# FFN up: products 1, 6, 7 and 4 add up in one accumulator pair, with ScalarE copies of the states between

## Chip, core, metric

One core of one Trainium2 chip runs the whole program in one launch. The metric is device microseconds of that core; the time of a kernel is the median of its runs. All five engines have their own instruction stream and wait for one another by semaphores: TensorE (PE in the profile) multiplies, VectorE (DVE), ScalarE (ACT), GpSimd (POOL) and SyncE (SP), which here only issues DMAs.

## The reference, cut to what matters

Two layers of a decoder trunk with 512 tokens and 1024 features, all in float32. Each layer is a mixer of four branches, which is not touched, and then the feed-forward network (FFN) with 2816 hidden features:

```python
hf = rmsnorm(x, norm_ffn)
gate, up = jnp.split(hf @ ffn_w_up, 2, axis=-1)
return x + (jax.nn.silu(gate) * up) @ ffn_w_down
```

The change lies in `hf @ ffn_w_up`: (512 x 1024) times (1024 x 5632), and in the silu and the product behind it.

## The kernel before

**Precision.** A float32 product is made of three TensorE matmuls, `mm3` (lines 306, 307, 308): each operand is split into hi and lo, and hi·hi, lo·hi and hi·lo are added. The weights are split on the core: ScalarE copies the raw float32 weights into `w_hi` (line 118, the helper of all activations), VectorE subtracts that from them into `w_lo` (line 1212 in the FFN, line 270 elsewhere).

**Products.** The up projection is not made of eight block products (two halves of the tokens by two halves of the features by gate and up) but of seven, in the manner of Strassen and Winograd, on sums of blocks. The inputs are `h` (`h_hi`, `h_lo`) and sums of its blocks, `sx` (`s_hi`, `s_lo`, whose lo is made on line 1134). The weight blocks are summed too: a `Block` is loaded by SP (line 1188), a second matrix is added to it by an accumulating DMA on GpSimd's queue (line 1193) or by VectorE (`plus`, line 1203). The hidden features are taken in six groups q, five of 512 columns and a last one of 256. Of each group:

- `X` begins as gate weights plus up weights of the even rows, `Y` as the up weights of the odd rows. X plus Y feeds p6, and later, with the gate weights of the odd rows (`w`) added to it, p4. Y alone feeds p3; with the even rows' up weights added to it by DMA it feeds p7. X at first feeds p5.
- p1 takes the gate weights of the even rows, p2 those of the odd rows, `w`.

A product is 24 matmuls: two token blocks t, four row blocks k, three of `mm3`, in two halves of two k each, since a weight block is split in two pieces (four pieces are kept, `W_BUFS`, and three raw buffers `w_raw`, `RAW_BUFS`; two more raw buffers `f_raw` belong to the FFN's own pool and take the place of the mixer's memory).

**Accumulators.** The FFN has four pairs of PSUM banks: A, B, C, and tr for transposes. The products of a group run p1, p6, p3, p2, p7, then the transposes of the first two token blocks' result (`turn`, on line 1264, with a VectorE part on line 1268), then p5 of the next group, then p4. p1 and p2 add up in A; p6, p7 and p4 in B; p5 and p3 in C (in the last group p4 uses C). VectorE makes the sums that leave PSUM (`plus` on line 1359): p1 plus C into e, p1 plus B into u, u plus C, e plus B, and p1 plus B behind p4; ScalarE copies p1 out once (into d1). u and e are the up parts; gate parts go through ScalarE's silu, with the norm's factor as its scale, and VectorE multiplies (`silu_mul`, line 1329).

**Order.** The program is written in the order above, but a scheduler with a simulated timeline puts each engine's instructions in their order when the program is built; weight splits and the additions behind products have a raised priority. After groups 2 and 5 the down projection takes the groups so far (`a_hi`, `a_lo`).

Of the kernel before, what the change touches and what calls it, by code (L numbers as in the profile page):

```python
# [16 lines left out]
AF = mybir.ActivationFunctionType  # L17
OP = mybir.AluOpType
# [52 lines left out]
def hybrid_trunk(ctx: ExitStack, tc: tile.TileContext, x, mem, positions, norm_mix, w_in, conv_w,  # L71
# [92 lines left out]
    ps = tr_ps()  # L164
# [1053 lines left out]
    def ffn(l, h, sx, ssq, xr, spare, late):  # L1218
# [2 lines left out]
        widths = [512] * (FF // 512) + [FF % 512]  # L1221
        Q = len(widths)
        ends = {2: (0, 3), Q - 1: (3, Q)}
        HS = S // 2
        A11, S1, A12, A22, S3, S2, S4 = ((h, 0, 0), (h, 0, HS), (h, 1, 0), (h, 1, HS), (sx, None, 0), (sx, None, HS),
                                         (sx, None, 2 * HS))

        with tc.tile_pool(name="ffn", bufs=1) as fp:
            a = (fp.tile([P, 12, S], F32R, name="a_hi"), fp.tile([P, 12, S], F32R, name="a_lo"))
            norm = {}  # L1230

            def block(n, name="w_raw"):
                if name == "w_raw":
                    t = wpool.tile([P, 2048], F32, name="w_raw", bufs=RAW_BUFS)
                else:
                    t = fp.tile([P, 2048], F32, name=name, bufs=2)
                return Block(t[:, :4 * n].rearrange("p (k n) -> p k n", n=n), n)

            def gate_w(q):
                return up[:, q * 512:q * 512 + widths[q]]  # L1240

            def up_w(q):
                return up[:, FF + q * 512:FF + q * 512 + widths[q]]

            def product(pss, form, parts, first, mid=None):
                src, odd, s0 = form
                n = parts[0][0].shape[2]
                for i, (hi, lo) in enumerate(parts):
                    for t in range(2):
                        for k in range(2):  # L1250
                            kk = 2 * i + k
                            c = kk if odd is None else 2 * kk + odd
                            mm3(pss[t][:, :n], pair(src, c, slice(s0 + t * P, s0 + (t + 1) * P)),
                                (hi[:, k, :], lo[:, k, :]), first and kk == 0, kk == 3, not first)
                    if i == 0 and mid is not None:
                        mid()

            def turn(tiles, t0, q):
                n = widths[q]
                base = 4 * (q % 3)  # L1260
                for t, src in enumerate(tiles):
                    ps = tr_ps()
                    for i in range(n // P):
                        pe.transpose(ps[:, i * P:(i + 1) * P], src[:, i * P:(i + 1) * P], ident)  # L1264
                    ps = ps[:, :n].rearrange("p (a b) -> p a b", b=P)
                    hi, lo = (x[:, base:base + n // P, (t0 + t) * P:(t0 + t + 1) * P] for x in a)
                    A(hi, ps, AF.Copy)
                    dve.tensor_sub(lo, ps, f(hi))

            def tmps(i, n):  # L1270
                return [spare[:, 2 * i + t, :n] for t in range(2)]

            def accs(name):
                return [bank[name]() for _ in range(2)]

            st = {}

            def first_sum(q):
                urgent = ()
                if q:  # L1280
                    moves = st[q - 1]["Y"].moves
                    urgent = (moves[2:], order) if q == 1 else (moves[:2], landed)
                if q == 0:
                    st[q] = {"B11": block(widths[q]).load(gate_w(q), 0), "X": block(widths[q])}
                else:
                    st[q] = {"X": block(widths[q], "f_raw")}
                st[q]["X"].load(gate_w(q), 0).add(up_w(q), 0, *urgent)

            def p5(q):
                d = st[q]  # L1290
                d["C"] = accs("C")
                product(d["C"], S1, d["X"].split(*zip(*st[q - 1]["g"]) if q else ()), True)

            def p1(q, mid=None):
                d = st[q]
                d["A"] = accs("A")
                w = d["B11"] if q == 0 else block(widths[q]).load(gate_w(q), 0)
                product(d["A"], A11, w.split(), True, mid)

            def p6(q):  # L1300
                d = st[q]
                d["B"] = accs("B")
                d["Y"] = block(widths[q]).load(up_w(q), 1)
                d["X"].plus(d["Y"])
                product(d["B"], S2, d["X"].split(), True)

            def p3(q):
                d = st[q]
                product(d["C"], S4, d["Y"].split(), False)
                d["Y"].add(up_w(q), 0)  # L1310

            def p2(q):
                d = st[q]
                w = block(widths[q], "w_raw" if q else "f_raw").load(gate_w(q), 1)
                product(d["A"], A12, w.split(), False)
                d["X"].plus(w)

            def p7(q):
                product(st[q]["B"], S3, st[q]["Y"].split(), False)

            def p4(q):
                d = st[q]
                if q == Q - 1:
                    d["C"] = accs("C")
                product(d["BC"[q == Q - 1]], A22, d["X"].split(), q == Q - 1)

            def silu_mul(dst, src, t, other):
                return (A(dst, src, AF.Silu, scale=norm["r"][:, t:t + 1]),
                        dve.scalar_tensor_tensor(dst, other, norm["n"][:, t:t + 1], dst, op0=OP.mult, op1=OP.mult))

            pending = []

            def flush():
                for args in pending:
                    turn(*args)
                pending.clear()

            def hi_prio():
                return tc.high_priority(offset=AHEAD)

            def down(q):
                g0, g1 = ends[q]
                f0, f1 = g0 * 512, min(g1 * 512, FF)
                kt = (f1 - f0) // P
                wd = ffn_w_down[l][f0:f1, :]
                end = q == Q - 1
                if last:
                    down_tokens(xr, wd, a, kt, end)
                    return None, None
                h2 = ssq2 = None  # L1350
                if end:
                    h2, ssq2 = new_h(), new_ssq()
                residual(lambda m: xr[:, m, :], wd, a, kt, 256, h2, ssq2, lambda c: g_mix(l + 1, c), spill=end)
                return h2, ssq2

            def plus(dst, src, ps, n):
                with hi_prio():
                    for t in range(2):
                        dve.tensor_add(dst[t], src[t], ps[t][:, :n])

            first_sum(0)
            for q in range(Q):
                n = widths[q]
                d1, e, u, g = (tmps(i, n) for i in ((0, 1, 2, 3) if q % 2 else (3, 1, 2, 0)))
                p1(q, flush)
                d = st[q]
                if q == 0:
                    p5(0)
                    late()
                    r = norm_token(ssq)  # L1370
                    nr = small(NT, name="nrstd_t", bufs=2)
                    dve.tensor_scalar(nr, r, -1.0, None, op0=OP.mult)
                    norm.update(r=r, n=nr)
                with hi_prio():
                    for t in range(2):
                        A(d1[t], d["A"][t][:, :n], AF.Copy)
                plus(e, d1, d["C"], n)
                p6(q)
                plus(u, d1, d["B"], n)
                p3(q)  # L1380
                if q + 1 < Q:
                    first_sum(q + 1)
                plus(u, u, d["C"], n)
                p2(q)
                d["g"] = [silu_mul(g[t], d["A"][t][:, :n], t, u[t]) for t in range(2)]
                p7(q)
                plus(e, e, d["B"], n)
                turn(g, 0, q)
                if q + 1 < Q:
                    p5(q + 1)  # L1390
                if q + 1 == Q:
                    plus(d1, d1, d["B"], n)
                p4(q)
                plus(d1, d1, d["BC"[q + 1 == Q]], n)
                for t in range(2):
                    silu_mul(d1[t], d1[t], t + 2, e[t])
                pending.append((d1, 2, q))
                if q in ends:
                    flush()
                    res = down(q)  # L1400
# [40 lines left out]
```

## Time and profile before

| what | value |
|---|---|
| median of 3 runs | 1996.49 us (1995.89 to 1996.67) |
| span of the profiled execution | 1994.9 us, granted TensorE clock 1.000 |
| the profiled execution against the runs | its span is 1.6 us below their median; the profile gives no time beyond the span |
| busy: TensorE, VectorE, ScalarE, GpSimd | 100%, 70%, 52%, 4% |
| the FFN of layer 0 in that span | about 682 to 968 us and the down projection's end behind it |
| the FFN of layer 1 | begins at about 1649 us |

In a timeline row stand the start in us, the busy us, the engine, the line, the operation, output and inputs, and the count; in brackets the idle time ahead of it and what ended it. In a group's row stand the count, the busy us and the mean ns of one, then the engine's idle time ahead of these instructions. A waits row has the total us, the number of times and the longest. TensorE's rows overlap, since matmuls are pipelined: what a matmul costs in a stream is the distance between two starts.

### The profile page before, as it was taken

What the parts mean: (1) busy time and instruction counts of PE and PEld (TensorE: products, weight loads), DVE (VectorE), ACT (ScalarE), POOL (GpSimd) and SP (SyncE); (2) the same over time, 40 slices, a digit from 0 to 9 for tenths busy, and PEclk for the clock granted to TensorE, in tenths of its full rate; (3) what the DMA queues carried; (4) which work ended last, traced back from release to release, by engine and by line L of the source; (5) the groups of instructions that cost most, each with busy time, mean ns of one, the idle gap of its engine ahead of it and who ended that gap; (6) DMA issues with size and microseconds to landing.
All of it is one profiled execution on the core that took longest, in us unless ns stands there. A gap on an engine that the chain in (4) does not pass through costs nothing.

```text
span 1994.9 us, 26474 instructions
## 1 busy us (share of the span) xinstructions
PE 1987.4 (100%) x10057; PEld 1669.8 (84%) x10057; DVE 1394.2 (70%) x2661; ACT 1033.3 (52%) x1795; POOL 69.9 (4%) x85
## 2 busy tenths in 40 slices
PE   9999999999999999999999999999999999999999
PEld 7898988778888888888889898877888888888897
DVE  7779997547666887458657889853677578854772
ACT  7653643666553645234555454366767455532551
POOL 1000000000000010000000000000000001100100
PEclk9999999999999999999999999999999999999999
DMA  9632223213234485353453223321322346643541
GB/s 314 208 106 75 76 88 103 67 53 104 66 99 144 114 202 138 116 148 75 131 165 95 81 63 96 95 85 53 96 85 76 118 145 171 152 143 106 116 128 53
DMA packets 172498, 226.86 MB, mean 114 GB/s; under 512 B 5954, under 2 KB 120212, under 8 KB 172372
## 3 DMA queue, kind: packets, MB, share of 16 engines
q1 hardware_dynamic: 155072, 193.55, 30.2%
q0 software_dynamic: 13344, 23.21, 7.2%
q10 hardware_dynamic: 3956, 8.42, 1.1%
q8 instruction: 79, 1.29, 0.3%
q14 instruction: 47, 0.39, 0.1%
HBM read 214.67 MB, written 10.49 MB: 113 GB/s over the span
## 4 chain that ended last, share of the span: by engine, by line
PE 98%; DMA 1%; ACT 0%; DVE 0%; SPq 0%; issue 0%; DVEq 0%; ACTq 0%
PE mm L306 19%; PE mm L307 19%; PE mm L308 18%; PE B L306 5%; PE B L307 5%; PE B L308 5%; PE A L308 4%; PE A L307 4%; PE A L306 4%; PE C L306 2%; PE C L307 2%; PE C L308 2%; PE tr L797 1%; PE tr L1264 1%; PE tr L791 1%; PE at L767 1%
## 5 line engine op out<-in xcount | busy, mean ns | idle before, releaser
L118 ACT ACTIVATE w_hi<-w_raw 128x1024 fp32r<-128x1024 f32 (+1 forms) x362 | 373.2, 1033 | 415.9 <-PE mm L307 149.4
L270 DVE TENSOR_TENSOR w_lo<-w_raw,w_hi 128x1024 fp32r<-128x1024 f32 x258 | 311.8, 1209 | 180.4 <-ACT w_hi L118 178.1
L306 PE MATMUL mm<-h_hi,w_hi 128*128 128x512 f32 x960 | 377.5, 394 | 1.3 <-DVE gate L596 0.9
L307 PE MATMUL mm<-h_lo,w_hi 128*128 128x512 f32 x960 | 377.0, 393 | 0.0
L308 PE MATMUL mm<-h_hi,w_lo 128*128 128x512 f32 x960 | 375.4, 392 | 0.0
L306 PEld LDWEIGHTS mm<-h_hi,w_hi 128*128 128x128 f32 x960 | 180.4, 188 | 39.1 <-DVE gate L596 1.3
L307 PEld LDWEIGHTS mm<-h_lo,w_hi 128*128 128x128 f32 x960 | 180.4, 188 | 36.7 <-issue 1.5
L308 PEld LDWEIGHTS mm<-h_hi,w_lo 128*128 128x128 f32 x960 | 180.4, 188 | 36.2 <-issue 0.2
L1212 DVE TENSOR_TENSOR w_lo<-w_raw,w_hi 128x1024 fp32r<-128x1024 f32 (+1 forms) x104 | 118.4, 1140 | 43.7 <-ACT w_hi L118 43.0
L306 PE MATMUL mm<-w_hi,h_hi 128*128 128x256 f32 (+2 forms) x384 | 116.3, 304 | 0.0
L307 PE MATMUL mm<-w_lo,h_hi 128*128 128x256 f32 (+2 forms) x384 | 116.2, 303 | 0.0
L308 PE MATMUL mm<-w_hi,h_lo 128*128 128x256 f32 (+2 forms) x384 | 116.1, 302 | 0.0
L308 PE MATMUL mm<-y_hi,w_lo 128*128 128x512 f32 x256 | 100.5, 393 | 0.0
L306 PE MATMUL mm<-y_hi,w_hi 128*128 128x512 f32 x256 | 100.3, 393 | 0.0
L307 PE MATMUL mm<-y_lo,w_hi 128*128 128x512 f32 x256 | 100.3, 392 | 0.0
L118 ACT ACTIVATE w_hi<-f_raw 128x1024 fp32r<-128x1024 f32 (+1 forms) x64 | 61.7, 977 | 50.5 <-PE B L308 42.0
L118 ACT ACTIVATE prob<-prob,small 128x128 f32<-128x128 f32 (+3 forms) x128 | 69.3, 556 | 33.0 <-DVE small L780 25.2
L1212 DVE TENSOR_TENSOR w_lo<-f_raw,w_hi 128x1024 fp32r<-128x1024 f32 (+1 forms) x64 | 70.9, 1121 | 14.9 <-ACT w_hi L118 14.7
L306 PEld LDWEIGHTS mm<-w_hi,h_hi 128*128 128x128 f32 x384 | 73.2, 191 | 3.0 <-issue 0.8
L308 PEld LDWEIGHTS mm<-w_hi,h_lo 128*128 128x128 f32 x384 | 73.4, 191 | 2.4
L307 PEld LDWEIGHTS mm<-w_lo,h_hi 128*128 128x128 f32 x384 | 73.2, 191 | 2.5
L307 PE MATMUL B<-w_lo,s_hi 128*128 128x512 f32 (+1 forms) x192 | 72.3, 377 | 0.0
(444 smaller groups left out, 4373.6 us busy)
## 6 DMA issues: line engine op xcount, KB each, us to landing
w_raw<-in_w_in_dram SPq DMA_DIRECT2D x72, 1024.0 KB, 5.2
w_raw<-in_ffn_w_up_dram SPq DMA_DIRECT2D x60, 512.0 KB, 4.8
w_raw<-in_ffn_w_down_dram SPq DMA_DIRECT2D x18, 1024.0 KB, 5.1
w_raw<-in_w_lift_dram SPq DMA_DIRECT2D x32, 512.0 KB, 3.4
w_raw<-in_ffn_w_up_dram POOLq DMA_DIRECT2D x24, 512.0 KB, 6.1
f_raw<-in_ffn_w_up_dram SPq DMA_DIRECT2D x20, 512.0 KB, 4.7
w_raw<-in_w_out_dram SPq DMA_DIRECT2D x8, 1024.0 KB, 5.0
f_raw<-in_ffn_w_up_dram POOLq DMA_DIRECT2D x16, 512.0 KB, 8.8
```

What stands on the lines that cost most here:

```text
L118: i = act.activation(dst, src, func, **kw)
L270: dve.tensor_sub(lo, raw[:, k:e], f(hi))
L306: pe.matmul(ps, ah, bh, start=first, stop=False, skip_group_check=go_on)
L307: pe.matmul(ps, ah, bl, start=False, stop=False, skip_group_check=go_on)
L308: return pe.matmul(ps, al, bh, start=False, stop=last, skip_group_check=go_on)
L767: pe.matmul(ps, q[:, hh, s], k[0][:, :n], start=True, stop=False)
L791: pe.transpose(pp[:, (2 * e + i) * P:(2 * e + i + 1) * P], probs[2 * i + e][:, b * P:(b + 1) * P], ident)
L797: pe.matmul(pv[e * HD:(e + 1) * HD, :], vt[:, b, :], pt[:, b, e * 2 * P:(e + 1) * 2 * P], start=b == 0, stop=b == t)
L1212: (dve.tensor_sub(lo, self.raw[:, 2 * i:2 * i + 2, :], f(hi)), dve_behind)):
L1264: pe.transpose(ps[:, i * P:(i + 1) * P], src[:, i * P:(i + 1) * P], ident)
```

## The change

The pair A and B become M and N, which swap roles in every group (`turns`, the sequence A B B A): p1, p6, p7 and, except in the last group, p4 all add into M; p2 alone goes to N, and stands directly behind p1 (behind p1 and p5 in group 0). What a sum needs of M between two products is copied out by ScalarE (`leave`): g behind p1, u behind p6, and e is a copy of C behind p5. VectorE then adds N to g, C to u and M to e. The silu of the other two token blocks reads M itself behind p4. In the last group M is copied to d1 and p4 goes to C. `less` and `sets` are new too, but nothing uses the first, and the second is empty. VectorE's sum of X and `w` moves from behind p2 to behind p3. Numbers of instructions in the program: TensorE 9770 in both, ScalarE 1715 and 1767, VectorE 2567 and 2519; those of GpSimd and SP are unchanged. Line numbers behind the inserted lines shift: 1264 to 1265, 1268 to 1269, 1329 to 1334, 1359 to 1369.

```diff
+            turns = cycle("ABBA")
...
+            def own(q):
+                return q == Q - 1 or q in sets
...
             def p1(q, mid=None):
                 d = st[q]
-                d["A"] = accs("A")
+                d["M"] = accs(next(turns))
                 w = d["B11"] if q == 0 else block(widths[q]).load(gate_w(q), 0)
-                product(d["A"], A11, w.split(), True, mid)
+                product(d["M"], A11, w.split(), True, mid)
+
+            def p2(q):
+                d = st[q]
+                d["N"] = accs(next(turns))
+                d["w"] = block(widths[q], "w_raw" if q else "f_raw").load(gate_w(q), 1)
+                product(d["N"], A12, d["w"].split(), True)
 
             def p6(q):
                 d = st[q]
-                d["B"] = accs("B")
                 d["Y"] = block(widths[q]).load(up_w(q), 1)
                 d["X"].plus(d["Y"])
-                product(d["B"], S2, d["X"].split(), True)
+                product(d["M"], S2, d["X"].split(), False)
 
             def p3(q):
                 d = st[q]
                 product(d["C"], S4, d["Y"].split(), False)
                 d["Y"].add(up_w(q), 0)
-
-            def p2(q):
-                d = st[q]
-                w = block(widths[q], "w_raw" if q else "f_raw").load(gate_w(q), 1)
-                product(d["A"], A12, w.split(), False)
-                d["X"].plus(w)
+                d["X"].plus(d["w"])
 
             def p7(q):
-                product(st[q]["B"], S3, st[q]["Y"].split(), False)
+                product(st[q]["M"], S3, st[q]["Y"].split(), False)
 
             def p4(q):
                 d = st[q]
-                if q == Q - 1:
+                if own(q):
                     d["C"] = accs("C")
-                product(d["BC"[q == Q - 1]], A22, d["X"].split(), q == Q - 1)
+                product(d["C" if own(q) else "M"], A22, d["X"].split(), own(q))
...
+            def leave(dst, ps, n):
+                with hi_prio():
+                    for t in range(2):
+                        A(dst[t], ps[t][:, :n], AF.Copy)
...
-                with hi_prio():
-                    for t in range(2):
-                        A(d1[t], d["A"][t][:, :n], AF.Copy)
-                plus(e, d1, d["C"], n)
+                leave(e, d["C"], n)
+                leave(g, d["M"], n)
+                p2(q)
                 p6(q)
-                plus(u, d1, d["B"], n)
+                plus(g, g, d["N"], n)
+                leave(u, d["M"], n)
                 p3(q)
                 if q + 1 < Q:
                     first_sum(q + 1)
                 plus(u, u, d["C"], n)
-                p2(q)
-                d["g"] = [silu_mul(g[t], d["A"][t][:, :n], t, u[t]) for t in range(2)]
+                d["g"] = [silu_mul(g[t], g[t], t, u[t]) for t in range(2)]
                 p7(q)
-                plus(e, e, d["B"], n)
+                plus(e, e, d["M"], n)
                 turn(g, 0, q)
-                if q + 1 < Q:
+                if own(q):
+                    leave(d1, d["M"], n)
+                else:
                     p5(q + 1)
-                if q + 1 == Q:
-                    plus(d1, d1, d["B"], n)
                 p4(q)
-                plus(d1, d1, d["BC"[q + 1 == Q]], n)
+                if own(q):
+                    plus(d1, d1, d["C"], n)
                 for t in range(2):
-                    silu_mul(d1[t], d1[t], t + 2, e[t])
+                    silu_mul(d1[t], d1[t] if own(q) else d["M"][t][:, :n], t + 2, e[t])
```

More of the change, by code (lines that the diff above doesn't have):

```diff
@@ L1223, in ffn @@
         ends = {2: (0, 3), Q - 1: (3, Q)}
+        sets = ()
         HS = S // 2
@@ L1359, in plus, with less @@
                         dve.tensor_add(dst[t], src[t], ps[t][:, :n])
+            def less(dst, src, ps, n):
+                with hi_prio():
+                    for t in range(2):
+                        dve.scalar_tensor_tensor(dst[t], src[t], -1.0, ps[t][:, :n], op0=OP.mult, op1=OP.subtract)
             first_sum(0)
```

## The prediction

> **What bounds the kernel now.** I read the page's busy shares, then the chain that ended last, then the waits of TensorE.
>
> ```profile
> PE 1987.4 (100%) x10057; PEld 1669.8 (84%) x10057; DVE 1394.2 (70%) x2661; ACT 1033.3 (52%) x1795; POOL 69.9 (4%) x85
> ...
> PE 98%; DMA 1%; ACT 0%; DVE 0%; SPq 0%; issue 0%; DVEq 0%; ACTq 0%
> ...
> core 0: 1994.9 us, clock 1.000
> ...
> PE tr L166 <- DVE ones_d L140: 1.1, 1, 1.1
> PE mm L306 <- DVE gate L596: 0.9, 1, 0.9
> ```
>
> TensorE is busy for the whole span and is 98% of the chain. Its waits (total, times, longest) are set-up and mixer lines; the accumulators A, B and C of the FFN do not occur. So the change can win almost nothing, and each wait that it puts before a product counts in full.
>
> One product's price is read from the starts of TensorE's rows:
>
> ```profile
> 695.19 0.39 PE L306 MATMUL B<-w_hi,s_hi 128*128 128x512 f32 x1
> ...
> 699.49 0.39 PE L308 MATMUL B<-w_hi,s_lo 128*128 128x512 f32 x1
> ...
> 950.44 0.28 PE L308 MATMUL A<-w_hi,h_lo 128*128 128x256 f32 x1
> ...
> 952.60 0.28 PE L308 MATMUL A<-w_hi,h_lo 128*128 128x256 f32 x1
> ```
>
> The first two rows are 19 starts apart, 0.226 us each: a product of 24 takes 5.43 us, its half 2.72. The last two are 18 starts apart, 0.12 us each: 2.88 us for a product of the 256-wide group.
>
> **The arithmetic that moves.** Group rows of layer 0's FFN (busy, mean ns):
>
> ```profile
> L1212 DVE TENSOR_TENSOR w_lo<-w_raw,w_hi 128x1024 fp32r<-128x1024 f32 x42 | 51.1, 1223 | 15.8 <-ACT w_hi L118 15.3
> L1359 DVE TENSOR_TENSOR merged<-merged,B 128x512 f32<-128x512 f32 x30 | 19.9, 681 | 3.6 <-PE B L308 3.5
> L1212 DVE TENSOR_TENSOR w_lo<-w_raw,w_hi 128x512 fp32r<-128x512 f32 x8 | 5.5, 687 | 1.7 <-ACT w_hi L118 1.7
> L1203 DVE TENSOR_TENSOR w_raw<-w_raw,f_raw 128x1024 f32<-128x1024 f32 x2 | 2.4, 1218 | 0.0
> ...
> L118 ACT ACTIVATE w_hi<-w_raw 128x1024 fp32r<-128x1024 f32 x67 | 70.8, 1059 | 108.7 <-PE C L308 27.7 <-PE A L307 27.1 <-PE B L307 23.1
> L118 ACT ACTIVATE w_hi<-w_raw 128x512 fp32r<-128x512 f32 x12 | 7.6, 631 | 15.7 <-PE A L307 4.4 <-PE B L307 4.4 <-PE C L308 3.0
> L118 ACT ACTIVATE merged<-A 128x512 f32<-128x512 f32 x10 | 5.9, 596 | 4.3 <-PE A L308 4.3
> ```
>
> Per layer ScalarE gets 4 more copies in each of five wide groups and 6 in the last; VectorE loses 4 additions in every group. The 40 wide additions of both layers are 40 x 0.681 = 27 us less VectorE, the 40 wide copies 40 x 0.596 = 24 us more ScalarE. With shares of 70% and 52% neither is on the path: 0. TensorE's matmuls are the same number: 0.
>
> The new order makes the pair M change hands: p6 waits for the copy of g, p7 for that of u, p4 for the sum e, and the next p2 for the silu that reads M. Between each pair of users stands one whole product (p2, p3, p5, the next p1), 5.43 us, against two copies of 0.6 or two additions of 0.68: 0, with at most 1 us a layer at the hand-over to the down projection, where a copy must end before the first matmul.
>
> **Layer 0, first group: p2 comes next.** Order on TensorE behind the norm's row sums, before (A and C hold p1 and p5, B is p6):
>
> ```order
> L350 MATMUL tr<-ones_d,ssq 128x1 x4
> L306 MATMUL B<-w_hi,s_hi 128x512 x2
> L306 MATMUL A<-w_hi,h_hi 128x512
> L307 MATMUL A<-w_lo,h_hi 128x512
> L306 MATMUL A<-w_hi,h_hi 128x512
> L307 MATMUL A<-w_lo,h_hi 128x512
> ```
>
> And after, from the last matmuls of p5 (B is p2):
>
> ```order
> L306 MATMUL C<-w_hi,h_hi 128x512
> L307 MATMUL C<-w_lo,h_hi 128x512
> L308 MATMUL C<-w_hi,h_lo 128x512
> L306 MATMUL B<-w_hi,h_hi 128x512 x2
> L307 MATMUL B<-w_lo,h_hi 128x512
> L308 MATMUL B<-w_hi,h_lo 128x512
> ```
>
> Where p6 stood, with weights long in place, p2 now follows the last of p1 and p5. Its weights lie in f_raw, which cannot be loaded before the mixer's last s_lo:
>
> ```profile
> 690.61 0.95 PE L350 MATMUL tr<-ones_d,ssq 128*128 128x1 f32 x8
> 691.41 0.72 PE L306 MATMUL B<-w_hi,s_hi 128*128 128x512 f32 x2
> ...
> 687.34 1.22 DVE L1212 TENSOR_TENSOR w_lo<-w_raw,w_hi 128x1024 fp32r<-128x1024 f32 x1
> 690.54 1.23 DVE L1212 TENSOR_TENSOR w_lo<-w_raw,w_hi 128x1024 fp32r<-128x1024 f32 x1
> 691.68 1.02 DVE L1134 TENSOR_TENSOR s_lo<-gate,s_hi 128x512 fp32r<-128x512 f32 x2
> ...
> 693.50 0.20 ACT L118 ACTIVATE small<-small 128x4 f32<-128x4 f32 x1
> 694.71 1.09 ACT L118 ACTIVATE merged<-A 128x512 f32<-128x512 f32 x2 [1.00 <-PE A L308]
> ...
> 692.78 13.35 SPq L1188 DMA_DIRECT2D f_raw<-in_ffn_w_up_dram  x6
> ...
> DMA to landing us min/median/max: 3.8/4.3/4.7
> ```
>
> The queue's load goes out at 692.78, right behind s_lo; the last row is for its two halves. The two w_lo are p6's. VectorE's order there, before:
>
> ```order
> L1212 TENSOR_TENSOR w_lo<-w_raw,w_hi 128x1024
> L1131 TENSOR_TENSOR h_lo<-gate,h_hi 128x512
> L1127 SCALAR_TENSOR_TENSOR gate<-gate 128x256
> L1131 TENSOR_TENSOR h_lo<-gate,h_hi 128x512
> L1128 SCALAR_TENSOR_TENSOR gate<-gate 128x256
> L1212 TENSOR_TENSOR w_lo<-w_raw,w_hi 128x1024
> L1134 TENSOR_TENSOR s_lo<-gate,s_hi 128x512
> ```
>
> And after, from the same second h_lo:
>
> ```order
> L1131 TENSOR_TENSOR h_lo<-gate,h_hi 128x512
> L1128 SCALAR_TENSOR_TENSOR gate<-gate 128x256
> L1134 TENSOR_TENSOR s_lo<-gate,s_hi 128x512
> L1134 TENSOR_TENSOR s_lo<-gate,s_hi 128x256
> L231 SCALAR_TENSOR_TENSOR small<-tr,small 128x4
> L232 SCALAR_TENSOR_TENSOR rstd_t<-small 128x4
> L1387 TENSOR_SCALAR nrstd_t<-rstd_t 128x4
> L1212 TENSOR_TENSOR w_lo<-f_raw,w_hi 128x1024 x2
> L1212 TENSOR_TENSOR w_lo<-w_raw,w_hi 128x1024 x2
> L1203 TENSOR_TENSOR w_raw<-w_raw,f_raw 128x1024 x2
> L1212 TENSOR_TENSOR w_lo<-w_raw,w_hi 128x1024
> ```
>
> Now s_lo has no split ahead of it; behind it come p2's two, p6's two, the two sums X plus w, and the split of Y for p3. So the load goes at about 692.78 - 2 x 1.22 = 690.3 and lands at 694.1. ScalarE is at its small norm until 693.7, then copies A (1.09, to 694.8), then w_hi (1.06, to 695.9); w_lo ends at 697.1. TensorE has 12 matmuls behind the row sums (691.41), until 694.1. It waits 1.7 us for w_hi, does two matmuls, and waits 0.8 for w_lo: 2.5 us. If w_hi comes before the copies it is 1.8; if the load stays at 692.78, 4.3. I take 2.5, since both splits are gone in the order.
>
> The clock was 1.000 throughout, and the longest wait in the rows above is 1.1 us. The Trainium skill (TensorE: Matmul & The Clock Gate, Part 1) says that TensorE falls to half its clock after an idle window of about 3.4 us; no run here shows such a gap, and only the upper end of 4.3 would reach it, adding by that page an estimated 1.7 us, which the sum does not need.
>
> **Layer 1, first group.**
>
> ```profile
> 1657.81 1.90 SPq L1188 DMA_DIRECT2D f_raw<-in_ffn_w_up_dram  x4
> ...
> DMA to landing us min/median/max: 3.6/4.1/4.6
> ...
> 1660.66 0.95 PE L350 MATMUL tr<-ones_d,ssq 128*128 128x1 f32 x8
> 1661.47 0.47 PE L306 MATMUL B<-w_hi,s_hi 128*128 128x512 f32 x1
> ```
>
> Here p2 stands behind the row sums, at 1661.47. One split less ahead of s_lo: load at 1656.6, landed 1660.2, w_hi 1661.3, w_lo 1662.5. Two matmuls run to 1661.9, then 0.6 of waiting (0.3 to 1.8, the upper end with the load where it was).
>
> **Y's accumulation.** Before, p2 stood between p3 and p7; the transfer that adds to Y, which can go only after p3's split, has one product less to land in.
>
> ```profile
> DMA to landing us min/median/max: 6.0/6.7/7.5
> ...
> DMA to landing us min/median/max: 5.9/6.0/6.1
> ...
> 733.29 0.39 PE L306 MATMUL B<-w_hi,s_hi 128*128 128x512 f32 x1
> ...
> 736.22 1.19 POOL L1193 DMA_DIRECT2D w_raw<-in_ffn_w_up_dram  x1 [14.57 <-DVE w_lo L1212]
> 738.55 1.20 POOL L1193 DMA_DIRECT2D w_raw<-in_ffn_w_up_dram  x1 [1.15 <-DVE w_lo L1212]
> ...
> DMA to landing us min/median/max: 6.2/6.4/6.5
> ...
> DMA to landing us min/median/max: 4.5/4.9/5.3
> ...
> DMA to landing us min/median/max: 10.2/10.4/10.5
> ```
>
> The landings are, in order: Y in layer 0's first group, in layer 1's, in the second group, in the 256-wide group, and the next X in the first group, which queues behind Y's.
>
> *Second to fifth groups.* With p6's start as T, the halves go at T+2.9 and T+5.3, and land at T+9.1 and T+11.8. With w_hi and w_lo (2.28) that is T+11.4 and T+14.1. p7 now starts at T+10.9; its first two matmuls need only w_hi, so it needs the w_lo at T+11.3 and T+14.0: just in time, and here the splits stand earlier, behind p2: 0.
>
> *First groups.* In layer 0 VectorE reaches p2's second w_lo at 699.2 (ScalarE copies C first); five more of 1.22 end at 705.3. Y's half lands 6.0 later, w_lo is ready at 713.6. TensorE: 70 matmuls from 697.1, 712.9, and two of p7, 713.4: 0.2 us (to 1.7 at a landing of 7.5). In layer 1 the second w_hi stands behind three copies, a sum and a further copy come between, and Y's split ends near 1672.2: landed 1678.1, w_hi 1679.2, w_lo 1680.4, against 1662.5 + 15.9 = 1678.4. It waits 0.8 and 0.75: 1.5 (0 to 2.5). Behind them the next X lands some 4 us after Y, for p5: 0.5 in each layer (0 to 2.0).
>
> *256-wide groups.* p6 and p3 last 5.8 us together. Split at T, landed T+4.9, w_hi and w_lo 1.32: T+6.2, 0.3 late with the first two matmuls; the second half, a half product later and queued, 0.75 more: 1.05 a layer (0 to 2.5).
>
> **Sum.** 2.5 + 0.6 + 0.2 + 1.5 + 2 x 0.5 + 2 x 1.05 = 7.9 us on the profiled execution's span of 1994.9. The median of the runs, 1996.5, lies 1.6 above that span; I add to it: 2004.4 us. The lower ends give 2.1, the upper ones 4.3 + 1.8 + 1.7 + 2.5 + 4 + 5 + 2 = 21.3.
>
> **Rivals.**
> - *The transfers are hidden.* Plain loads of Y's size land faster:
>
> ```profile
> w_raw<-in_ffn_w_up_dram SPq DMA_DIRECT2D x60, 512.0 KB, 4.8
> ```
>
> If the additions did so too, the first groups' p7 would lose 1.2 of 1.5, p5 nothing, the narrow groups some 0.4 each, and with p2 at its lower ends the sum is 1.8 + 0.3 + 0.3 + 1.3 = 3.7: 2000.2, no change that a measurement can tell (0.2% is 4 us). Against it: every addition's row is 5.9 or more at full width. Chance 0.29. The Trainium skill (DMA: Bandwidth & Descriptors, Anatomy of one DMA) gives 2.0 us plus bytes over 436 GB/s, an estimate of 3.2 us here; the trace has 5.9 to 7.5 for it, so the measurement decides and the rule does not carry this rival.
> - *Every group's p7 waits.* Eight wide groups are just covered at 6.2 to 6.5. It decides once the additions land 2 us later, and X's rows of 10.4 show how far queueing goes; 1.5 each is 12 more, 2016. For it: the cover is one product less in every group. Chance 0.16.
> - *Faster.* The waits on L596 and like lines go because layer 1's rows shift: at most the 2.0 us of the rows quoted first, 1994.5, within 0.2%. Against it: nothing of the mixer's order on TensorE changes. Chance 0.05.
> - That the order is not really changed is excluded by the rows above.
>
> **How the numbers follow.** The forecast, 2000.5 to 2010, has 0.50. Slower by over 0.2%: that and the 0.16, less 0.01 of the first that ends below 2000.5, 0.65. Faster by over 0.2%: no row gives 4 us, so 0.03, for what I do not see. Within: the rest, 0.32. The range runs from 1996.5, the forecast's lower ends less the faster case, to 2013, which takes in about half of the way to the upper ends; it leaves out the faster case and most of the one at 2016, 0.2 in all.
>
> **What would show it.** Right: TensorE waiting about 2.5 us for w_lo and w_hi of f_raw near 695, 0.6 near 1662, 1.5 near 1679 for w_raw's, and about 1 in each 256-wide group; none in groups two to five; granted clock 1.000. Wrong: no waits on L306 or L307 for f_raw, landings of Y's additions under 5 us, or a p7 that waits in every group.

## The result, and the profile after

| | before | after |
|---|---|---|
| median of 4 runs each | 1996.58 us | 2010.8 us (2009.88 to 2012.2) |
| ratio | 1 | 1.0072 [1.0058, 1.0086] |
| span of the profiled execution | 1994.9 us | 2008.3 us |

The change costs 14.2 us by the medians and 13.4 us by the two spans. Two of the four runs show a mean granted clock of 1.000 (2009.99 and 2009.88 us, the first is the profiled one), two of 0.999 (2012.2 and 2011.62 us). One of the eleven runs of e2_no_yadd below was slow, 2472.45 us at a granted clock of 0.752; the range and the ratio given there leave it out.

The page's busy shares and the cores' row of the kernel after, to be laid beside the first fence of the prediction:

```profile
PE 1991.8 (99%) x10057; PEld 1669.5 (83%) x10057; DVE 1367.8 (68%) x2613; ACT 1055.0 (53%) x1847; POOL 69.9 (3%) x85
...
core 0: 2008.3 us, clock 1.000
```

VectorE has 26 us less to do and ScalarE 22 us more, near the 27 and 24 of the prediction's count, and TensorE has the same number of matmuls. The chain that ended last can be followed back only to about 1907 us, so that its shares do not compare with the 98% of before; but it runs now through a transfer where it ran through TensorE alone. Four consecutive pieces of it (start, us, what), in layer 1's last group:

```profile
1937.61 4.43 DMA w_raw<-in_ffn_w_up_dram
1942.12 0.64 ACT w_hi L118
1942.78 0.70 DVE w_lo L1212
1943.53 0.39 PE B L307
```

Transfer, split, product: nothing lies between them. How often that happens stands in TensorE's waits (total, times, longest):

```profile
PE B L306 <- ACT w_hi L118: 4.8, 5, 2.1
PE B L307 <- DVE w_lo L1212: 2.0, 5, 0.5
...
PE A L307 <- DVE w_lo L1212: 1.1, 2, 0.5
PE C L306 <- ACT w_hi L118: 1.0, 1, 1.0
...
PE A L306 <- ACT w_hi L118: 0.2, 1, 0.2
```

The rows with accumulators A, B and C did not occur before. Each waits for a weight piece (`w_hi`, `w_lo`), none directly for an accumulator, a copy or an addition behind a product. They are 9.1 us in all, less than the 13.4 by which the span grew, because idle time begins where the modelled end of the matmul before lies; the stall counts from start to start.

TensorE's timeline at the first group of layer 0 (p2, then p7), at the first group of layer 1 (p2, then p7 with a p5 matmul inside it), at the last group of layer 0 (p7), and at p5 of layer 0's first group:

```profile
693.52 0.39 PE L308 MATMUL C<-w_hi,h_lo 128*128 128x512 f32 x1
695.13 0.73 PE L306 MATMUL B<-w_hi,h_hi 128*128 128x512 f32 x2 [1.23 <-ACT w_hi L118]
696.39 0.50 PE L307 MATMUL B<-w_lo,h_hi 128*128 128x512 f32 x1 [0.52 <-DVE w_lo L1212]
696.73 0.40 PE L308 MATMUL B<-w_hi,h_lo 128*128 128x512 f32 x1
...
712.77 0.73 PE L306 MATMUL A<-w_hi,s_hi 128*128 128x512 f32 x2 [0.22 <-ACT w_hi L118]
714.03 0.50 PE L307 MATMUL A<-w_lo,s_hi 128*128 128x512 f32 x1 [0.53 <-DVE w_lo L1212]
...
1670.33 0.73 PE L306 MATMUL B<-w_hi,h_hi 128*128 128x512 f32 x2 [0.34 <-ACT w_hi L118]
1671.59 0.50 PE L307 MATMUL B<-w_lo,h_hi 128*128 128x512 f32 x1 [0.53 <-DVE w_lo L1212]
...
1688.92 0.50 PE L307 MATMUL A<-w_lo,s_hi 128*128 128x512 f32 x1 [0.53 <-DVE w_lo L1212]
...
1692.97 0.50 PE L306 MATMUL C<-w_hi,h_hi 128*128 128x512 f32 x1 [0.99 <-ACT w_hi L118]
...
970.03 0.50 PE L306 MATMUL B<-w_hi,s_hi 128*128 128x256 f32 x2 [0.52 <-ACT w_hi L118]
970.75 0.38 PE L307 MATMUL B<-w_lo,s_hi 128*128 128x256 f32 x1 [0.23 <-DVE w_lo L1212]
...
720.50 0.50 PE L307 MATMUL C<-w_lo,h_hi 128*128 128x512 f32 x1
```

The first rows show how one stall is counted. The start at 693.52 should be followed by one at 693.75 and comes at 695.13: 1.38 us. Two matmuls are 0.45 of work, the third starts 1.26 after the first: 0.81. The next start follows after 0.34 instead of 0.23: 0.11. That makes 2.30 us for this p2. Layer 1's p2 stands behind the row sums, which begin at 1669.04; in the kernel before the first product began 0.81 behind them (1660.66 and 1661.47 in the prediction), here 1.29.

And one place where nothing was forecast, between the two halves of p7 of layer 0's fourth group, whose second half needs the second half of Y:

```profile
901.65 0.39 PE L308 MATMUL B<-w_hi,s_lo 128*128 128x512 f32 x1
904.13 0.73 PE L306 MATMUL B<-w_hi,s_hi 128*128 128x512 f32 x2 [2.09 <-ACT w_hi L118]
905.39 0.50 PE L307 MATMUL B<-w_lo,s_hi 128*128 128x512 f32 x1 [0.53 <-DVE w_lo L1212]
```

Counted so, with the time by which TensorE's starts lie further apart than in the undisturbed stream:

| place | forecast, us | measured, us |
|---|---|---|
| layer 0, first group, p2 | 2.5 | 2.30 |
| layer 0, first group, p7 | 0.2 | 1.30 |
| layer 0, first group, p5 | 0.5 | 0.43 |
| layer 0, fourth group, p7 | 0 | 3.17 |
| layer 0, last group, p7 | 1.05 | 1.27 |
| layer 1, first group, p2 | 0.6 | 1.39 |
| layer 1, first group, p7 | 1.5 | 0.98 |
| layer 1, first group, p5 | 0.5 | 1.27 |
| layer 1, last group, p7 | 1.05 | 1.40 |
| sum | 7.9 | 13.5 |

The sum agrees with the 13.4 us by which the span grew, within what nine readings of some 0.1 us allow. (The second half of layer 0's last p7 loses some 0.3 more, which is not counted.)

What the piece itself waited for is mostly the transfer: in six of the nine places ScalarE's w_hi begins within 0.1 us of the landing and w_lo follows directly. In three, other work stood in between:

- Layer 0's p2: the load, issued at 689.77, landed after 3.6 us, at 693.4, but ScalarE first copied A out (693.07 to 694.13) and began w_hi at 694.02.
- Layer 1's p2: the load landed at about 1668.75 (issued at 1665.07, 3.7 us), and w_hi began at 1669.22, which its row puts down to TensorE.
- Layer 0's p5: X had landed and w_hi was done at 717.96, but VectorE was at a sum and a product of the silu (717.84 to 719.30) and began w_lo only at 719.22.

By these rows at most about 1.5 us of the 13.5 (an estimate: 0.65 + 0.47 + 0.43) comes from other work on ScalarE, VectorE and TensorE in front of a split. Copies of A, sums and products of this kind stand in the kernel before too; no run separates their share.

### The profile page after: what moved, and what is told of

Same layout as the page of the kernel before. It is cut to its first block, busy times and chain, and to the rows that moved or that the text cites. A ratio compares the mean times of both kernels' runs of the same rounds, so it can differ in the third digit from the quotient of the medians.

```text
span 2008.3 us, 26428 instructions
## 1 busy us (share of the span) xinstructions
PE 1991.8 (99%) x10057; PEld 1669.5 (83%) x10057; DVE 1367.8 (68%) x2613; ACT 1055.0 (53%) x1847; POOL 69.9 (3%) x85
## 3 DMA queue, kind: packets, MB, share of 16 engines
q8 instruction: 79, 1.29, 0.3%
## 5 line engine op out<-in xcount | busy, mean ns | idle before, releaser
L596 DVE TENSOR_TENSOR gate<-mm,rstd 128x512 f32<-128x512 f32 x64 | 44.0, 687 | 25.5 <-PE mm L308 25.4
```

The source lines that it names most:

```text
L596: dve.tensor_mul(g, ps, r_b)
```

## The experiments

Two theories. **Late transfers:** all of the loss is weight pieces that land later against the product that needs them: `w` of the first groups (p2 comes one place earlier), Y's accumulating transfer (one product less to land in), and what queues with it. **Copies and hand-overs:** one pair that holds four products makes TensorE, ScalarE and VectorE hand PSUM to each other more often, and that costs time between the waits, which the waits only take over. The first theory says that the new accumulators are free in the old order, and that the waits go with their transfers; the second says that the loss stays with the accumulators.

### The transfers taken away

**e1_w0_raw.** In the first group `w` gets a raw buffer that is free early, and Y takes the late one:

```diff
-                d["w"] = block(widths[q], "w_raw" if q else "f_raw").load(gate_w(q), 1)
+                d["w"] = block(widths[q]).load(gate_w(q), 1)
...
-                d["Y"] = block(widths[q]).load(up_w(q), 1)
+                d["Y"] = block(widths[q], "w_raw" if q else "f_raw").load(up_w(q), 1)
```

> The changed kernel, but in group 0 p2's weights lie in a w_raw buffer, which is loaded long before, and Y in the f_raw buffer. Theory (waits for late weights): p2's waits in group 0 go (2.3 us in layer 0, 1.3 in layer 1 by the changed kernel's trace), the other waits stay: about 2007.5, between 2006 and 2009. Rival (the ScalarE copies and the hand-overs of the accumulator pair cost the time): p2 into the other pair stays late, 2010.8.

2009.48 us (2008.02 to 2012.99), ratio to the kernel before 1.0067 [1.0055, 1.008]: hardly better than the change. The waits of p2 are gone in both layers, but in layer 0 p7 of the same group now waits instead. TensorE's rows there, and the windows around them (us, busy and matmuls, granted clock, DMA share, GB/s):

```profile
709.83 0.39 PE L308 MATMUL C<-w_hi,s_lo 128*128 128x512 f32 x1
712.07 0.73 PE L306 MATMUL A<-w_hi,s_hi 128*128 128x512 f32 x2 [1.85 <-ACT w_hi L118]
713.33 0.50 PE L307 MATMUL A<-w_lo,s_hi 128*128 128x512 f32 x1 [0.53 <-DVE w_lo L1212]
...
710.77:714.18 3.41, 1.58 (x6) 1.00 1.12 213
714.18:717.59 3.41, 3.41 (x11) 0.50 1.14 208
```

TensorE came to p7 over 2 us earlier, at 710 and not at 712.4, and the sum in Y lands only 0.6 us sooner: GpSimd issued its first half 2.0 us earlier (702.42 against 704.40), but it took 8.5 us to land and not 7.2, with a load of SP's issued 0.5 us behind it. The start is at 712.07, against 712.77 in the change. A wait was taken away, and the next late transfer took its place: this p7 now loses 2.9 us where it lost 1.3. On top the granted clock fell to 0.50 for 3.4 us, in which the matmuls start 0.43 us apart and not 0.227. The two runs at a clock of 1.000, 2008.02 and 2008.48 us, lie in the expected 2006 to 2009; the other three, at 0.999 and 0.998, lie above.

**e2_no_yadd** leaves out the accumulating transfer into Y, so that p7 multiplies by Y alone:

```diff
                 product(d["C"], S4, d["Y"].split(), False)
-                d["Y"].add(up_w(q), 0)
...
-                    urgent = (moves[2:], order) if q == 1 else (moves[:2], landed)
+                    urgent = () if q == 1 else (moves[:2], landed)
```

> The changed kernel without the accumulating transfer into Y in all groups; p7 multiplies Y as p3 had it, so its output is not the reference's. Theory: all waits of p7 go (1.3 + 3.2 + 1.1 in layer 0, 0.9 + 1.2 in layer 1) and those of p5 behind it (0.4 + 1.3): 9.3 less, about 2001.5, with 3.6 left for p2 in group 0. Rival (copies and hand-overs): the copy of u still stands between p6 and p7, 2010 or a little less.

2000.4 us (1999.33 to 2001.81), ratio 1.0018 [1.0009, 1.0027], 1.1 us below what was expected. Of TensorE's FFN waits only p2's are left:

```profile
PE B L306 <- ACT w_hi L118: 1.5, 2, 1.2
...
PE B L307 <- DVE w_lo L1212: 1.1, 2, 0.5
```

So the waits of p7 and p5 in all groups, some 10 of the 14 us (9.8 by the table above), hang on that one kind of transfer. Taking it away also takes its traffic off the DMA engines, so this run alone does not say how the transfer delays them.

**e3_both** makes both edits.

> Both edits together (no accumulating transfer into Y, p2's weights of group 0 in w_raw). Theory: no wait in the FFN up is left, 1996.5 to 1999: the new accumulators themselves cost nothing and gain nothing. Rival (copies and hand-overs): 2005 or more.

1996.94 us (1996.72 to 1997.14), ratio 1.0001 [0.9992, 1.001]. With the two kinds of late weights gone, the new accumulators, the new copies and the new order cost nothing that a run can tell; and with 24 accumulating transfers fewer and no wait in the FFN but one of 0.4, there is no gain either. The bound is the stream of matmuls. This ends the second theory as far as it needs the time to stay.

### Order and accumulators taken apart

**e4_before_p2_first** is the kernel before, with its accumulators and VectorE additions, and only p2 moved ahead of p3:

```diff
                 plus(u, d1, d["B"], n)
+                p2(q)
                 p3(q)
                 if q + 1 < Q:
                     first_sum(q + 1)
                 plus(u, u, d["C"], n)
-                p2(q)
```

> The kernel before with its own accumulators and additions, only p2 moved ahead of p3 (p1 p6 p2 p3 p7), so that p7 follows p3 as in the changed kernel. Theory: p7's waits for Y's accumulating transfer appear here too, in the first groups about 1 each and in the 256-wide groups about 1.1 each: 2000.5, with the wait in group 3 of layer 0 up to 2004. Rival (copies and hand-overs): nothing of theirs is in it, 1996.5.

2003.04 us (2001.59 to 2006.48), ratio 1.003 [1.0018, 1.0041]. Waits for weight pieces come with the order alone:

```profile
PE B L306 <- ACT w_hi L118: 3.4, 2, 1.9
...
PE C L306 <- ACT w_hi L118: 0.9, 1, 0.9
```

They are not where the expectation had them: the two of the first row are p7 of layer 0's first group and p7 of layer 1's last group, the third is p5 of layer 0's first group; the other first and last group lose under 1 us each, and no fourth group waits. The order is also not the whole of the change's: p2 stands behind p6 and not behind p1, so p2's own waits (3.7 us in the change) cannot occur here, and the sum of X and `w`, which belongs to p2 in this kernel, moves ahead with it.

**e6_old_all** is the opposite: the change's accumulators and copies, with the products in the order of before (p1, p6, p3, p2, p7). Shared edit of the next runs, here with `early = False`:

```diff
                 leave(g, d["M"], n)
-                p2(q)
+                if early:
+                    p2(q)
                 p6(q)
-                plus(g, g, d["N"], n)
+                if early:
+                    plus(g, g, d["N"], n)
...
                 plus(u, u, d["C"], n)
+                if not early:
+                    p2(q)
+                    plus(g, g, d["N"], n)
+                d["X"].plus(d["w"])
```

(`plus` of X and `w` leaves p3 for this place.)

> The changed kernel's accumulators and copies with the order of before in all groups (p1 p6 p3 p2 p7). Theory: no p7 waits for Y's accumulating transfer, since p2 stands between again, and the waits in group 0 and group 3 go as well; only p6's wait for the copies of p1 is new, and the scheduler puts p3's first matmuls ahead of it: 1997 to 2000. Rival (copies and hand-overs): the copies stand between p1 and p6, about 1 us in each of 12 groups, 2006 or more.

1997.78 us (1997.0 to 1999.3), ratio 1.0006 [0.9997, 1.0014], and no A, B or C in TensorE's waits. The two runs together are the cut: a part of the new order without the accumulators costs 6, the accumulators without the order cost nothing measurable (1.0 us by the medians, inside the interval). The new order includes the place of VectorE's sum of X and `w`, which this run puts back with p2.

### Place by place

**e5_old_q0** has the order of before in the first group of each layer alone (`early = q`).

> The changed kernel with the order of before in group 0 of both layers only (p1 p6 p3 p2 p7, the sum of X and w behind p2); the accumulators stay the new ones. Theory: the waits of that group go (by the changed kernel's trace 2.3 + 1.3 + 0.4 in layer 0, 1.3 + 0.9 + 1.3 in layer 1, 7.5 in all), up to 0.5 a layer comes back where p6 now waits for the copy of p1: 2003.3 to 2004.3. Rival (copies and hand-overs): p6 directly behind p1 waits longer, no gain, 2010.

2005.43 us (2002.98 to 2007.11), ratio 1.0045 [1.0031, 1.0058]. The median is above what was expected, and the runs part by clock: 2002.98 and 2003.91 at 1.000, against 2005.43, 2006.88 and 2007.11 at 0.999 and 0.998. The first two lie at the expectation (one inside, one 0.3 below), 6 to 7 us less than the change's runs at 1.000. In the profiled one (2002.98) TensorE's waits of the first groups are gone, and those of layer 0's fourth group and of the last groups are left:

```profile
PE B L306 <- ACT w_hi L118: 3.5, 3, 2.0
...
PE B L307 <- DVE w_lo L1212: 1.0, 3, 0.5
```

**e7_hold** goes for the wait that was not forecast. What happens in the change, by the timeline of VectorE, GpSimd and SP, ScalarE behind them, and the view of Y's tile in that window:

```profile
892.27 1.22 DVE L1203 TENSOR_TENSOR f_raw<-f_raw,w_raw 128x1024 f32<-128x1024 f32 x1
...
891.03 1.19 POOL L1193 DMA_DIRECT2D w_raw<-in_ffn_w_up_dram  x1 [25.14 <-DVE w_lo L1212]
892.76 1.20 POOL L1193 DMA_DIRECT2D w_raw<-in_ffn_w_up_dram  x1 [0.55 <-DVE w_lo L1212]
...
893.56 12.68 SPq L1188 DMA_DIRECT2D w_raw<-in_ffn_w_up_dram  x4
...
903.02 1.06 ACT L118 ACTIVATE w_hi<-w_raw 128x1024 fp32r<-128x1024 f32 x1 [5.27 <-DMA w_raw<-in_ffn_w_up_dram]
...
DMA to landing us min/median/max: 5.6/9.1/10.2
```

VectorE adds `w` to X (892.27, the last use of `w`'s buffer) now behind p3's split instead of behind p2. SP's load into that buffer, `w` of the fifth group, therefore goes out at 893.56, 0.8 us behind the second half of Y's addition, and that half, with the load beside it on the DMA engines, lands 10.2 us after its issue, at about 903. In the kernel before, SP's next load went out 4.6 us behind that half (887.27 and 882.70), which landed after 6.1; in layer 1's fourth group of the change it went out 2.1 us ahead of the first half (1863.70 and 1865.77), and the two halves landed after 5.7 and 6.9. The experiment keeps all else and lets that one load wait until Y's addition has landed:

```diff
                 d["w"] = block(widths[q], "w_raw" if q else "f_raw").load(gate_w(q), 1)
+                if q == 4:
+                    for m in d["w"].moves:
+                        for b in st[q - 1]["Y"].moves[2:]:
+                            tc.add_manual_dep(m.ins, b.ins.name, landed, reason="more urgent transfer")
```

> The changed kernel, but the load of w for group 4 waits until the accumulating transfer into Y of group 3 has landed; TensorE's order is the same. Theory: in layer 0 that transfer's second half took 10.2 us because this load went out 0.8 us behind it; without it it lands in about 6.2, and the 3.2 us of waiting in group 3 go: 2007.6. Rival (the accumulating transfers are late by themselves there): the wait stays, 2010.8.

2007.84 us (2007.46 to 2009.12), ratio 1.0056 [1.0043, 1.0069], 3.0 us less than the change, and the wait at the fourth group's p7 is gone. The same rows now (GpSimd, SP, the tile):

```profile
893.26 1.20 POOL L1193 DMA_DIRECT2D w_raw<-in_ffn_w_up_dram  x1 [0.55 <-DVE w_lo L1212]
...
900.27 3.12 SPq L1188 DMA_DIRECT2D w_raw<-in_ffn_w_up_dram  x4
...
DMA to landing us min/median/max: 5.8/6.3/6.8
```

**e8_ends_hold** joins the pieces: the order of before in the first and last group of each layer (`early = 0 < q < Q - 1`), the held load, and the change's order and accumulators in the eight wide groups between.

> The changed kernel with the order of before in the first and the last group of both layers and with the held load of the run before. Theory: all waits that the changed kernel's trace shows are gone (7.5 + 3.2 + 2.3 of 13.4), up to 1.5 comes back for p6 behind the copies: 1998 to 1999.5. Rival: the copies and hand-overs in the eight groups that keep the new order still cost, 2003 or more.

1996.73 us (1996.19 to 1997.38), ratio 1.0000 [0.9991, 1.0009]. TensorE's first waits (no A, B or C is among the rest) and the busy shares; the span is 1995.5 us at a granted clock of 1.000:

```profile
PE tr L166 <- DVE ones_d L140: 1.1, 1, 1.1
PE mm L306 <- DVE gate L596: 0.9, 1, 0.9
...
PE 1988.1 (100%) x10057; PEld 1670.3 (84%) x10057; DVE 1369.1 (69%) x2613; ACT 1054.9 (53%) x1847; POOL 69.8 (3%) x85
```

It came out below its expectation: of the 14 us nothing is left, and the eight wide groups between add nothing. No version beat the kernel before; where TensorE is busy for 100% of the span there was nothing to win.

## Why the prediction was right, and where its sum was not

The sign, the mechanism and the wide range (1996.5 to 2013) were right: slower by waits for late weight pieces, with TensorE the bound. The sum was too small: 2004.4 forecast, 2010.8 measured, just above the forecast's own band of 2000.5 to 2010 and nearer in number to the rival of 2016, whose mechanism did not happen. By its own steps:

- **Arithmetic and hand-overs at nothing:** right. e6_old_all and e8_ends_hold have all of both and no time that a run can tell; of the 1 us a layer that was allowed at the hand-over to the down projection, e8_ends_hold, with the median of before, shows nothing. What ScalarE's copies of A in front of p2's split cost was priced in p2's term and not here.
- **p2 of layer 0's first group, 2.5:** 2.30, by the way described, with ScalarE's norm and its copies of A in front of w_hi. SP's load left earlier, as the order said, and TensorE did two matmuls between the two waits.
- **Its p7, 0.2 (to 1.7):** 1.30. The failed number is the landing: I took 6.0 us from Y's rows and it took 7.2. The rows of GpSimd, SP and the tile show why it may have been so:

```profile
702.87 0.88 SPq L1188 DMA_DIRECT2D f_raw<-in_ffn_w_up_dram  x2
...
704.40 1.20 POOL L1193 DMA_DIRECT2D w_raw<-in_ffn_w_up_dram  x1 [45.31 <-DVE w_lo L1212]
...
DMA to landing us min/median/max: 7.2/7.3/7.5
```

  GpSimd issued the addition at 704.40 (I had 705.3), and a load of SP's was out 1.5 us ahead of it. That this load is the cause was not tried here.
- **Its p5, 0.5:** 0.43, near by luck. I expected X's landing to be late; X was in time, and VectorE's sum and product in front of the split made the wait (720.50 above).
- **Layer 1's first group, 0.6 + 1.5 + 0.5:** 1.39 + 0.98 + 1.27, 3.6 for 2.6. The p7 part was too high, the other two too low; in p5's case the scheduler had put its first matmul into the middle of p7 (1692.97 above), so that the wait for X came earlier than I had placed it.
- **The last groups, 1.05 each:** 1.27 and 1.40.
- **Groups two to five, 0:** this step failed, once in eight: 3.17 us. It reckoned with the landing of Y's addition as in the rows of before, 6.2 to 6.5, and looked only at what stood between issue and use on TensorE, VectorE and ScalarE. The sum of X and `w` was named as moved, but its price was looked for in VectorE's time, and not in what it frees: a buffer, and with it a load of SP's. e7_hold shows that this load is the whole of it: with the load held back the wait is gone. The other seven groups were covered, so the rival in which every p7 waits was wrong too, although its reason, that landings of 10 occur, was right at one place.
- **The rival of hidden transfers** needed additions that land like plain loads. The kernel after's rows of DMA issues (KB each, median us to landing) say otherwise:

```profile
w_raw<-in_ffn_w_up_dram SPq DMA_DIRECT2D x60, 512.0 KB, 4.5
w_raw<-in_ffn_w_up_dram POOLq DMA_DIRECT2D x24, 512.0 KB, 6.3
```

- **Clock 1.000:** so in the profiled execution and in one other, but the two runs at 0.999 lie 2 us higher and lift the median by about 0.9. The sum had no term for it: the prediction expected a fall of the clock only at a gap near 3.4 us, and gaps of about 2 us were enough in other runs (below).

The terms were 7.9 us for 13.5; of the 5.6 missing, 3.2 is the step that failed and the rest sizes.

## What to carry to other kernels

When TensorE is busy throughout, ask of a reordering not what each engine does more or less, but which weight has now one product less to arrive in, and count the late pieces place by place. Of every step that is moved on an idle engine, ask which buffer its last read frees, which load is waiting for that buffer, and beside which urgent transfer that load will now run. And when a wait is removed, look at the next transfer on the way before counting the gain: in e1_w0_raw 1.6 of p2's 2.3 us came back as a longer wait of p7.

## What the runs showed of the hardware

- **Y's accumulating transfers of 512 KB took 5.6 to 7.5 us to land in the kernel after, and one 10.2, with SP's loads issued 0.8 us behind it.** Holding the load back made it 6.8 (e7_hold). X's additions of that size, on the same GpSimd queue, took longer: a median of 8.0 us. The Trainium skill (DMA: Bandwidth & Descriptors, Anatomy of one DMA) gives 2.0 us plus bytes over 436 GB/s, an estimate of 3.2 us here; no addition of this size landed so soon.
- **The first two matmuls behind a wait start further apart:** 0.34 us (696.39 to 696.73 above) instead of 0.23. It comes at every one of the 512-wide waits above, 0.11 us each.
- **The granted clock can fall after waits of about 2 us.** In e1_w0_raw it was 0.50 for 3.41 us, after 1.85 and 0.53 us of idling. In e4_before_p2_first's profiled execution (2006.48 us), by TensorE's row and the two stretches of 3.41 us around it:

```profile
1937.68 0.77 PE L306 MATMUL B<-w_hi,s_hi 128*128 128x256 f32 x2 [1.93 <-ACT w_hi L118]
...
1934.33:1937.74 3.41, 1.48 (x13) 1.00 0.60 90
1937.74:1941.15 3.41, 3.41 (x15) 0.50 0.06 20
```

  In the kernel after, the wait of 2.09 us at 904.13 left it at 1.00, and so did one of 1.99 us in e5_old_q0 (the second row):

```profile
900.06:903.47 3.41, 1.98 (x9) 1.00 0.62 159
...
896.69:900.10 3.41, 1.60 (x8) 1.00 0.54 138
```

  The Trainium skill (TensorE: Matmul & The Clock Gate, Part 1) speaks of an idle window of about 3.4 us that runs freely and does not start with the kernel. The slow stretches here are that long, 3.41 us; but the idling that preceded them was shorter, 1.9 us in one piece. In every trace the clock changes a whole number of 3.41 us behind its first rise. Cut on that grid, the stretch ahead of a slow one had TensorE busy for 1.58 us (e1_w0_raw, above) and 1.48; those of 1.60 (e5_old_q0) and 1.98 (the kernel after) had no slow one behind them, and neither had one of 1.56 at the end of e4_before_p2_first (1999.18 to 2002.59). In both slow cases the stretch ahead was less than half busy, and one and the same gap can fall into one such stretch or be cut in two; but the busy time of the profile gives no threshold. What decides it was not tried and stays open.
